# Sparse attention's logits with keys made once per head: hi and lo parts stacked on the partitions

## The chip, the cores and the metric

The kernel runs on one core of one Trainium2 chip. The metric is the device time of one execution in microseconds (us). TensorE multiplies matrices, VectorE and ScalarE work on its results in PSUM and on tiles in SBUF, GpSimd (POOL) on tiles in SBUF, and SyncE (SP) issues the DMAs. Each engine works through its own list of instructions in order; semaphores tie the lists together.

## The reference, cut to what matters

One layer of an encoder: 2048 tokens, width 1024, float32. A projection feeds three mixers (a sparse attention, a gated linear attention, a window attention); their outputs go through an output projection, and a gated feed-forward layer follows. The change is in the sparse attention. It picks 256 keys for each query by an index score, and attends to these in a latent space of 128:

```python
c_kv = rms_norm(c_kv, kv_norm)                                  # 2048 x 128
q_lat = einsum('bshd,rhd->bshr', q, w_uk) * HEAD_DIM ** -0.5    # 4 heads, 64 -> 128
score = einsum('bqhs,bqh->bqs', relu(einsum('bqhd,bsd->bqhs', qi, k_idx)), wi)
_, sel = top_k(where(admissible, score, -inf), 256)             # blocks of 128 queries
logits = einsum('bqhr,bqkr->bhqk', q_lat, c_kv[sel]) + bias     # bias by distance, 4 heads
p = softmax(where(valid, logits, -inf))
o = einsum('bshr,rhd->bshd', einsum('bhqk,bqkr->bqhr', p, c_kv[sel]), w_uv)
```

A logit is thus q . (w_uk^T c): the query can be taken to the latents (q w_uk^T), or the latents to keys of 64 numbers per head (c w_uk).

## The kernel before, in words

Products that need nearly full precision are made of packed parts: a number x becomes hi (rounded to the packed type) and lo = x - hi, and a product is hi.hi + lo.hi + hi.lo, three matmuls into one PSUM tile. Plain float32 operands take two passes of TensorE and stream their columns at half the rate.

The tokens go in four groups of 512. `dense()` is one thread of work: `pass1` for each group (projections of the sparse attention's inputs), `pass2` for each group (the two other mixers), then the feed-forward layer for groups 0 and 1, one group at a time (PSUM tiles `mf`). `dsa()` is the other thread: for each of 16 blocks of 128 queries `select` finds the 256th largest score by bisection (VectorE and ScalarE in turns), and `attend` attends. `merge` interleaves both threads in program order by the costs that they yield: the one that lags by its share of its total is taken next. `dsa`'s total is `SPEED` times a sum over the blocks of the larger of `select_cost` and `attend_cost`. The framework then orders each engine's list by its own estimate, near program order. When both threads are done, the feed-forward layer runs for groups 2 and 3 together, seven half products in place of eight (PSUM tiles `pf`).

In `attend` of block qb the keys are 0 to (qb+1)*128. The query's part `qa` is loaded from DRAM (L1238), taken to the latents by four products of plain type (L1242), and split to `lh` and `ll`. Per head the keys go in strips of at most 512 columns; the last strip is 256 wide and takes the bias `near`, which POOL adds to the mask (L1257) from the resident table `near_s`; beyond 128 keys the bias is one number per head, which cancels. A strip is three products (L1264 to L1266) and one instruction on VectorE that adds the mask and takes the least (L1268). ScalarE takes the exponential (L1272), TensorE turns it (L1281), and sums with the values `cv` (L1291).

`cTh` and `cTl` hold the latents' hi and lo parts, 128 partitions x 2048 each, made in `pass1` (L803, L804). `pers` holds what lives through the sparse attention, `gl` what ends with `pass2`, and `f1` opens its pools when `pass2` has ended. Weights are split once into hi and lo (L114, L117), stored, and loaded again by later groups (`load_halves`, L129 and L142), through five or six tiles `w`.

Of the kernel before, what the change touches and what calls it, by code (L numbers as in the profile page):

```python
# [19 lines left out]
P = 128  # L20
# [16 lines left out]
C_ID, C_GLA, C_BIT, C_POW, C_SWA, C_CAUS, C_REV, NC_ = 0, 128, 256, 288, 320, 576, 832, 960  # L37
# [47 lines left out]
def hybrid_encoder_kernel(ctx, tc, xT, w_in, w_out, w_g, w_u, w_d, vec, wuk, wuv, wg2,  # L85
# [10 lines left out]
    qaD = [dram.tile([2, P, G], F32, name=f"qaD{g}") for g in range(NG)]  # L96
# [4 lines left out]
    bD = dram.tile([8, NREL], F32, name="bD")  # L101

# [80 lines left out]
    def ffn(groups, pools, ps_f, ps_n, n_raw, n_w, n_act, n_lead, before, prepare=iter(())):  # L183
# [306 lines left out]
        def gate_up(f):  # L490
# [5 lines left out]
            for i, hs in enumerate(halves):  # L496
# [86 lines left out]
    with ExitStack() as mx:  # L583
# [48 lines left out]
        cs = pers.tile([P, C_SWA], F32, name="cs")  # L632
        ident = cs[:, C_ID:C_ID + P]
        wuk_s = pers.tile([P, 4, P], F32, name="wuk_s")
        wuv_s = pers.tile([P, 256], F32, name="wuv_s")
        bits = pers.tile([P, 32], I32, name="bits")

        def constants():
            nc.sync.dma_start(out=cs, in_=cst[:, 0:C_SWA])
# [6 lines left out]
        cTh = pers.tile([P, S], F32R, name="cTh")  # L646
        cTl = pers.tile([P, S], F32R, name="cTl")
# [4 lines left out]
        nsink = gl.tile([P, 4], F32, name="nsink")  # L652
        bias_s = gl.tile([P, 4, 256], F32, name="bias_s")
        near_s = pers.tile([P, 4, 256], F32, name="near_s")

        def bias_tables():
# [17 lines left out]
            for h in range(0, 8, 2):  # L674
# [8 lines left out]
                if h < 4:  # L683
                    A.copy(near_s[:, h:h + 2, :], pt.rearrange("p (h k) -> p h k", h=2))
# [81 lines left out]
        def pass1(g):  # L766
# [22 lines left out]
            for j in range(2):  # L789
# [5 lines left out]
                if j == 0:  # L795
# [28 lines left out]
                nc.sync.dma_start(out=qaD[g][j], in_=t)  # L824
# [94 lines left out]
        def gla_mix(g, j, bx):  # L919

            qe, ke, kd, vt, dec = (bx[n] for n in ("qe", "ke", "kd", "vt", "dec"))
            for t2 in range(2):
                pa = ps_mm()
                for u in range(2):
# [6 lines left out]
                                in1=cs[:, C_GLA:C_GLA + P].unsqueeze(1).to_broadcast([P, 4, P]),  # L931
# [174 lines left out]
        def select(qb, res):  # L1106
# [38 lines left out]
            def col(nm, dt=F32, n=1):  # L1145
                return sp.tile([P, n], dt, tag=nm, name=nm)
# [37 lines left out]
            e0, st, ps2, up = col("e0"), col("st", F32, 32), col("ps2", F32, 32), col("up")  # L1184
# [48 lines left out]

        def attend(qb, res):
# [3 lines left out]
            nc.sync.dma_start(out=qa[:, 0:256].rearrange("p (j t) -> p j t", j=2),  # L1238
                              in_=qaD[g].rearrange("j p t -> p j t")[:, :, q0:q0 + P])
# [15 lines left out]
            def logits(hd):  # L1255
                near = sp.tile([P, 256], F32, tag="near", bufs=N_NEAR, name="near")
                Q.tensor_add(near[:, 0:nw], x[:, far:nk], near_s[:, hd, 256 - nw:256])  # L1257
                lg = lgs[hd] = big()

                least = sp.tile([P, 8], F32, tag="least", name="least")  # L1260
# [222 lines left out]
```

## Time and profile before

| | |
|---|---|
| median of 3 runs | 2905.21 us (2900.52 to 2906.05) |
| the profiled execution's own time | 2909.43 us |
| its span | 2907.7 us |
| TensorE busy, share of the span | 2716.1 us, 93% |
| VectorE, ScalarE, POOL busy | 61%, 43%, 28% |
| mean granted clock of TensorE | 0.969 |
| moved by DMA | 471.08 MB, mean 162 GB/s |

A row of the timeline has the start, the time that the instruction took, the engine, the line, the operation, the tiles out<-in, rows*columns of the array that it uses, the shape of the moving operand, and its count; behind it, in brackets, the engine's idle time before it and what ended that. Matmuls overlap, so the time between two starts is what one costs. PE is TensorE, PEld its weight loads.

### The profile page before, as it was taken

To read this page: it belongs to the slowest core of one execution; us is meant where nothing else is said; L and a number is where in the kernel's file an instruction comes from. 1 tells how busy PE (TensorE), PEld (TensorE's weight loads), DVE (VectorE), ACT (ScalarE), POOL (GpSimd) and SP (SyncE) were. 2 spreads that over 40 slices of the span, in tenths; PEclk is the share of its full clock that TensorE was granted. 3 is DMA by queue.
4 is the path that set the end of the run, shared out by engine and by line. 5 is a ranking of instruction groups with operands and counts; after the bars stand their busy time and mean duration, and the time that the engine had idled before them with its cause. 6 is when DMAs were issued, how large, how long until landed. Compare 5 with 4: busy or idle time off the path is not lost. (4 is left out here: it accounts for less than half of the span.)

```text
span 2907.7 us, 37058 instructions
## 1 busy us (share of the span) xinstructions
PE 2716.1 (93%) x13136; PEld 2132.4 (73%) x13136; DVE 1782.3 (61%) x3662; ACT 1245.6 (43%) x2168; POOL 819.6 (28%) x666
## 2 busy tenths in 40 slices
PE   7888999999999989998988998999998999999998
PEld 5666767676776767776766786878776888888886
DVE  3787787787776767466367464464446544444445
ACT  4555664556555645454354442342433211112113
POOL 3113421010100354544442300000123443445440
PEclk8999999999999999999999999999999999999999
DMA  7655544243332666666657443444573443334432
GB/s 250 195 179 191 183 131 146 93 144 111 104 122 92 228 205 216 241 204 224 218 202 260 157 164 126 153 138 145 182 258 116 142 138 117 110 127 131 136 102 102
DMA packets 191114, 471.08 MB, mean 162 GB/s; under 512 B 19945, under 2 KB 51601, under 8 KB 190929
## 3 DMA queue, kind: packets, MB, share of 16 engines
q1 hardware_dynamic: 190928, 468.71, 48.8%
q8 instruction: 104, 1.70, 0.2%
q14 instruction: 82, 0.66, 0.1%
HBM read 341.61 MB, written 127.02 MB: 161 GB/s over the span
## 5 line engine op out<-in xcount | busy, mean ns | idle before, releaser
L117 POOL TENSOR_TENSOR w<-raw,w 128x512 fp32r<-128x512 f32 x272 | 367.2, 1361 | 596.7 <-ACT w L114 562.9
L1169 ACT ACTIVATE jd<-x,c 128x384 bf16<-128x384 f32 (+13 forms) x224 | 292.9, 1307 | 301.0 <-DVE c L1196 238.7
L201 PE MATMUL mf<-al,w 128*128 128x512 f32 x832 | 330.2, 398 | 9.6 <-DVE al L259 5.0
L199 PE MATMUL mf<-ah,w 128*128 128x512 f32 x832 | 332.7, 400 | 6.4 <-ACT ah L278 2.6
L1171 DVE TENSOR_SCALAR_CACHE_REDUCE jd<-x,c 128x384 bf16<-128x384 f32 (+13 forms) x224 | 331.0, 1477 | 6.9 <-DVE c L1180 0.5
L200 PE MATMUL mf<-ah,w 128*128 128x512 f32 x832 | 328.7, 396 | 0.0
L114 ACT CAST w<-raw 128x512 fp32r<-128x512 f32 x272 | 165.2, 617 | 364.3 <-PE pf L527 190.8
L370 PE MATMUL pf<-al,w 128*128 128x512 f32 x616 | 242.6, 394 | 6.6 <-POOL al L293 3.5
L368 PE MATMUL pf<-ah,w 128*128 128x512 f32 x616 | 242.3, 393 | 5.7 <-ACT ah L292 5.7
L740 PE MATMUL mm<-hh,w 128*128 128x512 f32 x576 | 241.7, 420 | 4.3 <-issue 2.0
L369 PE MATMUL pf<-ah,w 128*128 128x512 f32 x616 | 241.7, 393 | 0.0
L741 PE MATMUL mm<-hh,w 128*128 128x512 f32 x576 | 232.8, 404 | 0.0
L742 PE MATMUL mm<-hl,w 128*128 128x512 f32 x576 | 231.4, 402 | 0.0
L201 PEld LDWEIGHTS mf<-al,w 128*128 128x128 f32 x832 | 159.2, 191 | 47.0 <-DVE al L259 5.5
L199 PEld LDWEIGHTS mf<-ah,w 128*128 128x128 f32 x832 | 159.7, 192 | 40.4 <-issue 4.9
L528 DVE TENSOR_TENSOR x<-x,pf 128x512 f32<-128x512 f32 (+1 forms) x184 | 121.5, 664 | 106.9 <-PE pf L527 106.0
L200 PEld LDWEIGHTS mf<-ah,w 128*128 128x128 f32 x832 | 159.5, 192 | 32.1
L525 PE MATMUL mf<-fh,w 128*128 128x512 f32 x352 | 143.5, 408 | 17.7 <-ACT fh L114 6.9
L117 POOL TENSOR_TENSOR fl<-u,fh 128x512 fp32r<-128x512 f32 x44 | 58.1, 1320 | 321.1 <-ACT fh L114 321.1
L370 PEld LDWEIGHTS pf<-al,w 128*128 128x128 f32 x616 | 117.1, 190 | 34.2 <-POOL al L293 5.3
L526 PE MATMUL mf<-fh,w 128*128 128x512 f32 x352 | 140.7, 400 | 1.4 <-POOL w L117 1.4
L525 PE MATMUL pf<-fh,w 128*128 128x512 f32 (+1 forms) x368 | 141.1, 384 | 0.0
(299 smaller groups left out, 5914.0 us busy)
## 6 DMA issues: line engine op xcount, KB each, us to landing
w<-w SPq DMA_DIRECT2D x622, 512.0 KB, 3.5
raw<-in_w_g_dram SPq DMA_DIRECT2D x88, 256.0 KB, 3.6
raw<-in_w_u_dram SPq DMA_DIRECT2D x88, 256.0 KB, 3.4
xk<-in_xT_dram SPq DMA_DIRECT2D x64, 256.0 KB, 3.1
raw<-in_w_in_dram SPq DMA_DIRECT2D x44, 256.0 KB, 3.7
raw<-in_w_d_dram SPq DMA_DIRECT2D x44, 256.0 KB, 3.7
m<-mixT SPq DMA_DIRECT2D x32, 256.0 KB, 3.2
x<-in_xT_dram SPq DMA_DIRECT2D x32, 256.0 KB, 5.3
```

Source lines behind the costliest of these rows:

```text
L117: Q.tensor_sub(lo, src, hi.bitcast(F32))
L199: T.matmul(ps, a, act[k][0], start=(first and k == ks[0]), stop=False)
L200: T.matmul(ps, b, act[k][0], start=False, stop=False)
L201: T.matmul(ps, a, act[k][1], start=False, stop=(last and k == ks[-1]))
L368: T.matmul(ps, x, b[0], start=first, stop=False)
L369: T.matmul(ps, y, b[0], start=False, stop=False)
L370: T.matmul(ps, x, b[1], start=False, stop=last)
L525: T.matmul(ps, hi[:, os_], ah[:, hs], start=(j == 0), stop=False)
L740: T.matmul(ps, a, hh, start=(k == 0), stop=False)
L741: T.matmul(ps, b, hh, start=False, stop=False)
L1169: A.activation(jd, xs, AF.Sign, scale=-1.0, bias=c[:, 0:1], accum_out=cnt)
L1171: V.tensor_scalar(out=jd, in0=xs, scalar1=c[:, 0:1], scalar2=0.0, op0=ALU.is_ge, op1=ALU.add, accum_out=cnt)
```

## The change

The keys are made once: in `pass1`, per group, two products of plain type take the normed latents `cn` to keys of two heads each (64 partitions a head). The hi part of a head's keys goes to 64 partitions and the lo part to the other 64 of the same tile, `kt`, 1536 columns a head; the last group's go through DRAM (`k3D`) to `kt3`, which is loaded once the pools of `pass2` are closed. The query stands twice on the partitions. A strip is then two products: `lh` (the query's hi part on all 128 partitions) with the stacked keys, which gives hi.hi and hi.lo in one, and `ll` with the 64 partitions of hi alone. The products of L1242 go. The table of the near bias goes to DRAM, and each head of each block loads its piece. Beside that, tiles: the constants are laid out anew, `wuk_s`, `wuv_s` and the causal mask move to `gl`, the gate's product reuses its tile `s`, the stored sums of weights take tiles of the common tag `w`, three small tiles of `select` have one buffer. The costs that `attend` yields are smaller. Block 12 and later ones wait in the program until `kt3` is there, and the feed-forward thread until all blocks have attended.

```diff
@@ bias_tables
-                    A.copy(near_s[:, h:h + 2, :], pt.rearrange("p (h k) -> p h k", h=2))
+                    nr = gen_tile("nr")
+                    A.copy(nr, pt)
+                    nc.sync.dma_start(out=nearD[h // 2], in_=nr)
@@ pass1
-                    A.copy(cTh[:, g0:g0 + G], cn)
-                    V.tensor_sub(cTl[:, g0:g0 + G], cn, cTh[:, g0:g0 + G].bitcast(F32))
                 yield 5.2 - PART
                 ps = yield from proj(CH_QA + j, h)
                 if j == 0:
+                    for j2 in range(2):
+                        pk = ps_tr()
+                        T.matmul(pk, wuk_s[:, j2 * P:(j2 + 1) * P], cn, start=True, stop=True)
+                        for u in range(2):
+                            hd = 2 * j2 + u
+                            k_ = kt[:, hd, g0:g0 + G] if g < NG - 1 else gen_tile("k3").bitcast(F32R)
+                            rh, rl = (slice(i * 64, i * 64 + 64) for i in (u, 1 - u))
+                            A.copy(k_[rh], pk[rh])
+                            V.tensor_sub(k_[rl], pk[rh], k_[rh].bitcast(F32))
+                            if g == NG - 1:
+                                nc.sync.dma_start(out=k3D[hd], in_=k_.bitcast(F32))
@@ summed_halves, gate_up
-                w = pool.tile([P, 1024], F32R, tag="ws", bufs=1, name="ws")
+                w = pool.tile([P, 1024], F32R, tag="w", bufs=N_W, name="ws")
...
-                u = ft.tile([P, 512], F32, tag="u", bufs=2, name="u")
-                V.scalar_tensor_tensor(out=u, in0=s, scalar=0.5, in1=pu, op0=ALU.mult, op1=ALU.mult)
-                split(u, ah[:, hs], al[:, hs])
+                V.scalar_tensor_tensor(out=s, in0=s, scalar=0.5, in1=pu, op0=ALU.mult, op1=ALU.mult)
+                split(s, ah[:, hs], al[:, hs])
@@ attend
-            pq = ps_sc()
-            for hd in range(4):
-                T.matmul(pq[:, hd * P:(hd + 1) * P], wuk_s[:, hd, :], qa[:, (hd // 2) * P:(hd // 2 + 1) * P],
-                         start=True, stop=True)
+            nc.sync.dma_start(out=qa4[0:64], in_=qsrc)
+            nc.sync.dma_start(out=qa4[64:128], in_=qsrc)
...
-            A.activation(lh, pq, AF.Copy, scale=0.125)
-            V.scalar_tensor_tensor(out=ll, in0=pq, scalar=0.125, in1=lh.bitcast(F32), op0=ALU.mult, op1=ALU.subtract)
+            A.activation(lh, qa, AF.Copy, scale=0.125)
+            for u in range(2):
+                r = slice(u * 64, u * 64 + 64)
+                V.scalar_tensor_tensor(out=ll4[r, u::2], in0=qa4[r, u::2], scalar=0.125,
+                                       in1=lh4[r, u::2].bitcast(F32), op0=ALU.mult, op1=ALU.subtract)
+            while nk > N_KT and not kt3:
+                yield None
...
-                Q.tensor_add(near[:, 0:nw], x[:, far:nk], near_s[:, hd, 256 - nw:256])
+                nc.sync.dma_start(out=near[:, 0:nw],
+                                  in_=nearD[hd // 2][:, (hd % 2) * 256 + 256 - nw:(hd % 2 + 1) * 256])
+                Q.tensor_add(near[:, 0:nw], near[:, 0:nw], x[:, far:nk])
...
-                    T.matmul(ps[:, 0:w], lh[:, qs], cTh[:, k0:k0 + w], start=True, stop=False)
-                    T.matmul(ps[:, 0:w], ll[:, qs], cTh[:, k0:k0 + w], start=False, stop=False)
-                    T.matmul(ps[:, 0:w], lh[:, qs], cTl[:, k0:k0 + w], start=False, stop=True)
+                    for c0, k_ in keys(hd, k0, w):
+                        c1 = c0 + k_.shape[1]
+                        T.matmul(ps[:, c0:c1], lh[:, qs], k_, start=True, stop=False)
+                        T.matmul(ps[:, c0:c1], ll[hi, qs], k_[hi], start=False, stop=True)
...
-                    yield 0.9 * w / 512.0
+                    yield 0.6 * w / 512.0
...
-            return (qb + 1) * (0.9 + 1.0) + 1.5
+            return (qb + 1) * (0.6 + 1.0) + 0.6
@@ dense
+                k3p = f1.enter_context(tc.tile_pool(name="f1k", bufs=1))
+                kt3.append(k3p.tile([P, 4, G], F32R, name="kt3"))
+                nc.sync.dma_start(out=kt3[0].bitcast(F32), in_=k3D.rearrange("h p t -> p h t"))
...
                 yield from end
+                while len(attended) < NB:
+                    yield None
```

`keys(hd, k0, w)` returns the pieces of a strip: the columns of `kt` before 1536, and those of `kt3` behind.

On TensorE, in the second single feed-forward group, the start of block 14 stands so before the change (`mf` are dense products, `sc` the sparse attention's):

```order
L1242 MATMUL sc<-qa,wuk_s 128x128 x4
L199 MATMUL mf<-ah,w 128x512
L200 MATMUL mf<-ah,w 128x512
L201 MATMUL mf<-al,w 128x512
L199 MATMUL mf<-ah,w 128x512
L1264 MATMUL sc<-cTh,lh 128x512
L200 MATMUL mf<-ah,w 128x512
L201 MATMUL mf<-al,w 128x512
L1265 MATMUL sc<-cTh,ll 128x512
L1266 MATMUL sc<-cTl,lh 128x512
```

Now the strips of the last block, in the same stage (L201 to L203 are the dense products' lines now):

```order
L203 MATMUL mf<-al,w 128x512
L1298 MATMUL sc<-kt,lh 128x512
L1299 MATMUL sc<-kt,ll 128x512
L1298 MATMUL sc<-kt,lh 128x512
L1299 MATMUL sc<-kt,ll 128x512
L201 MATMUL mf<-ah,w 128x512
L202 MATMUL mf<-ah,w 128x512
L1298 MATMUL sc<-kt,lh 128x512
L1299 MATMUL sc<-kt,ll 128x512
L203 MATMUL mf<-al,w 128x512
```

A strip is a pair now, L1298 of 128 rows and L1299 of 64, mostly with dense products ahead and behind.

At the end of that stage TensorE's list before has the last block's turns and sums right ahead of the next stage's first product (`pf`):

```order
L1281 MATMUL tr<-cs,big 128x128 x4
L1310 MATMUL tr<-cs,dena 4x128
L1291 MATMUL o<-pT,cv 64x128
L1316 MATMUL tr<-dT,cs 64x128
L1291 MATMUL o<-pT,cv 64x128 x7
L1316 MATMUL tr<-dT,cs 64x128 x3
L199 MATMUL pf<-ah,w 128x512
```

and now the stage's own last products (L526 to L528) and a norm:

```order
L526 MATMUL mf<-fh,w 128x512
L527 MATMUL mf<-fh,w 128x512
L528 MATMUL mf<-fl,w 128x512
L236 MATMUL tr<-rs,ones 128x512
L201 MATMUL pf<-ah,w 128x512
```

The last block's sums stand some 120 rows earlier, among dense products.

On SP, at the load of block 12's index query (`qf`), the list before is:

```order
L142 DMA w_10086<-w 128x1024
L132 DMA raw<-in_w_u_dram 128x512
L1122 DMA qf<-qiD_69 64x4x128
L1123 DMA qf<-qiD_69 64x4x128
L142 DMA w_10093<-w 128x1024
```

and now:

```order
L134 DMA raw<-in_w_u_dram 128x512
L1286 DMA near<-nearD_80 128x256
L1138 DMA qf<-qiD_69 64x4x128
L144 DMA w_9876<-w 128x1024
```

A load of the near bias stands among the loads (`raw`) and stores (L144) of weights.

## Rows read from the trace of the kernel before

**Rows 1.** The page's first part: engines' busy us, share of the span, instructions

```profile
PE 2716.1 (93%) x13136; PEld 2132.4 (73%) x13136; DVE 1782.3 (61%) x3662; ACT 1245.6 (43%) x2168; POOL 819.6 (28%) x666
```

**Rows 2.** Busy time by stretch: PE, PEld, DVE, ACT, POOL; granted clock, DMA share, GB/s

```profile
0.00:250.00 250.00, 212.00 (x916) 156.33 (x917) 158.83 (x427) 132.96 (x280) 57.02 (x60) 0.92 0.65 206
250.00:1000.00 750.00, 706.05 (x3768) 523.48 (x3768) 585.57 (x1528) 440.86 (x878) 134.05 (x129) 0.97 0.42 135
1000.00:1570.00 570.00, 520.14 (x2502) 413.91 (x2501) 348.53 (x646) 293.31 (x451) 252.21 (x196) 0.96 0.64 221
1570.00:2085.00 515.00, 487.75 (x2422) 392.43 (x2421) 276.51 (x490) 181.34 (x248) 63.32 (x54) 0.97 0.47 155
```

**Rows 3.** Waits of PE: who for whom, us in total, times, longest

```profile
PE tr L1281 <- ACT big L1272: 20.6, 10, 7.3
...
PE sc L1264 <- DVE least L1268: 14.6, 9, 3.0
```

**Rows 4.** Timeline of PE: strips of 512 and of 256 columns

```profile
2061.61 0.40 PE L1265 MATMUL sc<-cTh,ll 128*128 128x512 f32 x1
2061.84 0.39 PE L1266 MATMUL sc<-cTl,lh 128*128 128x512 f32 x1
...
2066.45 0.28 PE L1265 MATMUL sc<-cTh,ll 128*128 128x256 f32 x1
2066.57 0.28 PE L1266 MATMUL sc<-cTl,lh 128*128 128x256 f32 x1
```

**Rows 5.** Line L1264, one product per strip: ns min/median/max, starts, shapes

```profile
L1264 PE MATMUL sc<-cTh,lh x192: 222/384/1169, 65.9 to 2095.4; 128*128 128x256 f32 x88, 128*128 128x512 f32 x72, 128*128 128x384 f32 x24, 128*128 128x128 f32 x8
```

**Rows 6.** Timeline of PE: one block's query taken to the latents

```profile
2051.94 1.05 PE L1242 MATMUL sc<-qa,wuk_s 128*128 128x128 f32 x8
2052.75 0.48 PE L199 MATMUL mf<-ah,w 128*128 128x512 f32 x1
```

**Rows 7.** Timeline of PE: a product of plain type, 512 columns, two passes

```profile
1601.09 1.10 PE L234 MATMUL tr<-rs,ones 128*128 128x512 f32 x2 [3.19 <-DVE rs L228]
1602.02 0.31 PE L1281 MATMUL tr<-cs,big 128*128 128x128 f32 x1
```

**Rows 8.** Timeline of PE: a product of 64 rows between dense ones

```profile
567.03 0.40 PE L742 MATMUL mm<-hl,w 128*128 128x512 f32 x1
567.36 0.70 PE L1026 MATMUL sc<-kct,qc 64*128 64x256 f32 x2
567.98 0.50 PE L740 MATMUL mm<-hh,w 128*128 128x512 f32 x1
568.32 0.39 PE L741 MATMUL mm<-hh,w 128*128 128x512 f32 x1
```

**Rows 9.** Timeline of PE: four passes of plain type, 128 rows, 256 columns

```profile
957.02 1.03 PE L926 MATMUL mm<-qe,ke 128*128 128x256 f32 x4
957.88 0.38 PE L1281 MATMUL tr<-cs,big 128*128 128x128 f32 x2
```

**Rows 10.** DMA issues: count, size of each, median us to landing

```profile
qa<-qaD SPq DMA_DIRECT2D x16, 128.0 KB, 3.4
```

**Rows 11.** Line L1257, the near bias: its instructions, and who waited for it

```profile
L1257 POOL TENSOR_TENSOR near<-mk,near_s x64: 427/678/1127, 69.9 to 2069.3; 128x256 f32<-128x256 bf16 x60, 128x128 f32<-128x128 bf16 x4
...
  DVE big L1268: 0.7, 2
```

**Rows 12.** Line L804: ns min/median/max, starts

```profile
L804 DVE TENSOR_TENSOR cTl<-cn,cTh x4: 681/693/857, 39.2 to 224.9; 128x512 fp32r<-128x512 f32 x4
```

**Rows 13.** Timeline of PE: the end of the second single feed-forward group

```profile
2087.65 0.39 PE L527 MATMUL mf<-fl,w 128*128 128x512 f32 x1
...
2098.82 1.13 PE L1281 MATMUL tr<-cs,big 128*128 128x128 f32 x8 [1.90 <-ACT big L1272]
...
2111.38 0.47 PE L199 MATMUL pf<-ah,w 128*128 128x512 f32 x1 [1.03 <-POOL al L259]
```

**Rows 14.** Timeline of SP: the next stage's first weights

```profile
2090.56 1.75 SPq L129 DMA_DIRECT2D w<-w  x4
```

More of the change, by code (lines that the diff above doesn't have):

```diff
@@ L35 @@
 V_MIX, V_FFN, V_FIN, V_KVN, V_BG, V_GN, V_SINK, NV = 0, 8, 16, 24, 25, 27, 31, 35
-C_ID, C_GLA, C_BIT, C_POW, C_SWA, C_CAUS, C_REV, NC_ = 0, 128, 256, 288, 320, 576, 832, 960
+C_ID, C_BIT, C_POW, C_GLA, C_SWA, C_CAUS, C_REV, NC_ = 0, 128, 160, 192, 320, 576, 832, 960
 CH_QA, CH_QI, CH_C, CH_M = 0, 2, 4, 5
@@ L95, in hybrid_encoder_kernel @@
     mixT = [dram.tile([KC, P, G], F32, name=f"mixT{g}") for g in range(NG)]
-    qaD = [dram.tile([2, P, G], F32, name=f"qaD{g}") for g in range(NG)]
+    qaD = [dram.tile([4, 64, G], F32, name=f"qaD{g}") for g in range(NG)]
     qiD = [dram.tile([4, 64, G], F32, name=f"qiD{g}") for g in range(NG)]
@@ L101, in hybrid_encoder_kernel @@
     bD = dram.tile([8, NREL], F32, name="bD")
+    nearD = [dram.tile([P, 512], F32, name=f"nearD{j}") for j in range(2)]
+    k3D = dram.tile([4, P, G], F32, name="k3D")
     const = ctx.enter_context(tc.tile_pool(name="const", bufs=1))
@@ L630, in big @@
             return bigp.tile([P, S], F32, tag="big", name="big")
-        cs = pers.tile([P, C_SWA], F32, name="cs")
+        cs = pers.tile([P, C_SWA - P], F32, name="cs")
         ident = cs[:, C_ID:C_ID + P]
-        wuk_s = pers.tile([P, 4, P], F32, name="wuk_s")
-        wuv_s = pers.tile([P, 256], F32, name="wuv_s")
+        wuk_s = gl.tile([P, 256], F32, name="wuk_s")
+        wuv_s = gl.tile([P, 256], F32, name="wuv_s")
         bits = pers.tile([P, 32], I32, name="bits")
         def constants():
-            nc.sync.dma_start(out=cs, in_=cst[:, 0:C_SWA])
+            nc.sync.dma_start(out=cs, in_=cst[:, 0:C_SWA - P])
+            nc.sync.dma_start(out=causal, in_=cst[:, C_GLA:C_GLA + P])
             nc.sync.dma_start(out=wuv_s, in_=wuv)
@@ L645, in hybrid_encoder_kernel @@
         cv = pers.tile([P, NB, 256], F32, name="cv")
-        cTh = pers.tile([P, S], F32R, name="cTh")
-        cTl = pers.tile([P, S], F32R, name="cTl")
+        N_KT = (NG - 1) * G
+        kt = pers.tile([P, 4, N_KT], F32R, name="kt")
+        kt3 = []
         ks = pers.tile([P, S], F32R, name="ks")
@@ L652, in hybrid_encoder_kernel @@
         nsink = gl.tile([P, 4], F32, name="nsink")
+        causal = gl.tile([P, P], F32, name="causal")
         bias_s = gl.tile([P, 4, 256], F32, name="bias_s")
-        near_s = pers.tile([P, 4, 256], F32, name="near_s")
         def bias_tables():
@@ L823, in pass1 @@
                 V.tensor_mul(t, ps, rs)
-                nc.sync.dma_start(out=qaD[g][j], in_=t)
+                nc.sync.dma_start(out=qaD[g][2 * j:2 * j + 2].rearrange("u d t -> (u d) t"), in_=t)
                 yield 5.2 - PART
@@ L930, in gla_mix @@
                                 in0=pa.rearrange("p (b i) -> p b i", i=P),
-                                in1=cs[:, C_GLA:C_GLA + P].unsqueeze(1).to_broadcast([P, 4, P]),
+                                in1=causal.unsqueeze(1).to_broadcast([P, 4, P]),
                                 op=ALU.mult)
@@ L1143, in select, with col @@
             Q.memset(x[0:64, nk - 64:nk], LOW)
-            def col(nm, dt=F32, n=1):
-                return sp.tile([P, n], dt, tag=nm, name=nm)
+            def col(nm, dt=F32, n=1, bufs=2):
+                return sp.tile([P, n], dt, tag=nm, bufs=bufs, name=nm)
             xs = x[:, 0:nk]
@@ L1232, in select_cost, with keys @@
             return 4 * nk / 512.0 + 4.0 * nk / 960.0 + 9 * (nk / 960.0 + 0.4) + 23 * (nk / 1000.0 + 0.6)
+        def keys(hd, k0, w):
+            k1, r = k0 + w, []
+            if k0 < N_KT:
+                r.append((0, kt[:, hd, k0:min(k1, N_KT)]))
+            if k1 > N_KT:
+                a = max(k0, N_KT)
+                r.append((a - k0, kt3[0][:, hd, a - N_KT:k1 - N_KT]))
+            return r
         def attend(qb, res):
@@ L1237, in attend @@
             qa = att_tile("qa")
-            nc.sync.dma_start(out=qa[:, 0:256].rearrange("p (j t) -> p j t", j=2),
-                              in_=qaD[g].rearrange("j p t -> p j t")[:, :, q0:q0 + P])
-            pq = ps_sc()
-            for hd in range(4):
-                T.matmul(pq[:, hd * P:(hd + 1) * P], wuk_s[:, hd, :], qa[:, (hd // 2) * P:(hd // 2 + 1) * P],
-                         start=True, stop=True)
+            qa4, qsrc = qa.rearrange("p (h t) -> p h t", h=4), qaD[g].rearrange("h d t -> d h t")[:, :, q0:q0 + P]
+            nc.sync.dma_start(out=qa4[0:64], in_=qsrc)
+            nc.sync.dma_start(out=qa4[64:128], in_=qsrc)
             lh = sp.tile([P, 512], F32R, tag="lh", bufs=1, name="lh")
             ll = sp.tile([P, 512], F32R, tag="ll", bufs=1, name="ll")
-            A.activation(lh, pq, AF.Copy, scale=0.125)
-            V.scalar_tensor_tensor(out=ll, in0=pq, scalar=0.125, in1=lh.bitcast(F32), op0=ALU.mult, op1=ALU.subtract)
+            A.activation(lh, qa, AF.Copy, scale=0.125)
+            lh4, ll4 = (t.rearrange("p (h t) -> p h t", h=4) for t in (lh, ll))
+            for u in range(2):
[4 more added lines that the diff above has]
+                yield None
             x = res[0]
@@ L1452, in _layout @@
     vec[:, V_SINK:V_SINK + 4] = f["sinks"][0][None, :]
-    wuk = np.zeros((P, 4, P), np.float32)
-    for h in range(4):
-        wuk[(h % 2) * 64:(h % 2) * 64 + 64, h, :] = f["w_uk"][0][:, h, :].T
     cst, oh = _constants()
```

5 lines of the change are left out of this document (3 added, 2 removed).

## The prediction

> **What bounds the kernel now.** I read the page's first part first: TensorE is busy for 93% of the span, no other engine for more than 61% [rows 1]. Then busy time by stretch, over the four stages in which the sparse attention runs beside dense work (first projections, second projections, two single feed-forward groups): 85, 94, 91 and 95% [rows 2]. The waits of TensorE come third: the longest entry is 20.6 us in ten pieces [rows 3]. So up to 2085 us the end is set by how long TensorE's own list takes; a saving on another engine is worth nothing there, and a microsecond on TensorE about 0.93 us, the mean share of these stages (1926 of 2085 us). The last 820 us (the double feed-forward group) hold no edited instruction.
>
> I read TensorE's cost from start to start in the timeline, since the durations shown there overlap: 512 columns of the packed type take 0.23 us, 256 take 0.12 [rows 4].
>
> **The change part by part.**
>
> *The third logits product goes.* It stands once per strip, 192 times: 72 of 512 columns, 24 of 384, 88 of 256, 8 of 128 [rows 5], together 69,632 columns, or 136 times 512. 136 x 0.23 = 31.3 us of TensorE less. The second product now contracts 64 rows instead of 128. I give that no gain: its 512 columns still have to stream.
>
> *The query's way to the latents goes.* Four products per block showed as eight passes, from 2051.94 us to the next dense product at 2052.75: 0.81 us [rows 6]. 16 x 0.81 = 13.0 us less.
>
> *The keys per head are made.* Two products of plain type and 512 columns per group, eight in all. One such took 0.93 us (1601.09 to 1602.02) [rows 7]: 7.4 us more. So far TensorE has 36.9 us less to do.
>
> *The shape of the array alternates.* This is the term that decides. The first product of a strip has 128 rows, the second 64, and the next instruction has 128 again. The kernel before has a product of 64 rows in its window attention, L1026, amid dense ones, and [rows 8] prices the way there and back: L742 starts at 567.03, L1026 at 567.36, which is 0.33 instead of 0.23. Its two passes of 256 columns of plain type then last until 567.98, 0.62 us; two such passes of 128 rows cost 0.43 (four from 957.02 to 957.88) [rows 9], so 0.19 more for two, 0.10 for one. The product after next starts 0.34 after its forerunner, again 0.11 too late. So a strip that has dense work behind it pays 0.10 + 0.10 + 0.11 = 0.31 us, one followed at once by the next strip or by short passes about 0.20. Bounds: 0.20 for all, and 0.40 (all of the 1.29 us from 567.03 to 568.32, less 0.89 for the same work without it). In the new instruction order there are 200 pairs (eight of the 192 strips are cut in two where the keys change tile). About 110 have two dense products behind them, the others the next strip or short passes: 110 x 0.31 + 90 x 0.20 = 52 us; bounds 40 and 80. A strip of 512 columns saves 0.23 us and pays 0.20 to 0.31; one of 256 saves 0.12 and pays the same.
>
> The Trainium skill (TensorEngine Tiling (Array Packing), Key Properties) says that to change the tiling mode, as against the tile alone, drains TensorE. The trace agrees as far as the late starts of [rows 8] go. Read to the letter, each of 400 changes costs what a product is still busy beyond its start-to-start time, 0.39 - 0.23 = 0.16 us by [rows 4]: 64 us instead of 52, inside the bounds above.
>
> Net on TensorE: -36.9 + 52 = +15 us, with the bounds from +3 to +43; times 0.93 it is +14.
>
> *The bias near the diagonal comes from DRAM.* 64 loads of 128 KB, on SP's queue, among the weight loads. The nearest load, the query's, lands after 3.4 us [rows 10]. The add on POOL was waited for by 0.7 us in all before [rows 11], so it has room, and in the new order SP issues a load well ahead of its use. What SP now waits for is that VectorE has read the tile two heads back; behind it stand weight loads, whose five or six tiles hold more than 10 us of dense work each way (a tile feeds 12 products, 2.7 us). I count nothing for the 63 later loads. The first must wait until the table has gone to DRAM and back, two landings instead of none while VectorE waits: between 0 and 7 us, I take 2. The query's second copy (16 more loads of 128 KB) lies beside its first: 0. Should that cover go, each late load costs up to 3.4 us (see the rivals).
>
> *Copies in the first projections.* Per group, four casts on ScalarE and four subtractions on VectorE of 64x512 take the place of one each of 128x512. The removed subtraction took 0.69 us [rows 12]; with as long for each new one, it is 12 x 0.69 = 8 us on either engine. In the first stage these are busy 159 and 133 of 250 us, so I count 0; TensorE could wait for a PSUM tile, 1 us per group at most. For the last group the four results go through DRAM: their stores and one 1 MB load are far from use (the keys are read first in block 12, long after).
>
> *The edits of tiles* (one tile less after the gate product, the stored weight sums through the common weight tiles, single buffers for three small columns, the two waits in the program) have one answer: their readers are many microseconds away, and in the order the two waits never hold anything up, since block 12 comes well inside the first feed-forward group. 0, and 5 us either way at the start of the second feed-forward group, where the stored sums stand between the norms.
>
> *The end of the sparse attention.* Its steps are now counted as shorter, so it runs earlier against the dense work. Before, the last dense product of the stage starts at 2087.65 and the next at 2111.38 [rows 13], 23.7 us in which the last block stands alone, with one gap of 1.90 before its transposes; by what its passes take amid dense work I estimate a third of that stretch as lost, 8 us (bounds 1.9 and 23.7). In the new order the last block ends some 120 rows ahead of the next stage's first product, and that loss goes. But what is late next stands there too: the next stage's first weights wait on SP for the last square sum on VectorE, and were issued at 2090.56 [rows 14]; with a landing of 3.4 us or more, TensorE would stand from 2087.9 to about 2094.5 with only a norm product to do. 8 lost before, 7 after: -1 us.
>
> **Sum.** 14 + 2 - 1 = +15 us. I take off 4 us, for drains that fall where TensorE would wait for VectorE anyway (14.6 us of [rows 3] stand before a strip's first product). The profiled execution took 2909.4 us, so 2920; the median of the runs is 4.2 us below the profiled one: 2916 us.
>
> **The rivals.**
>
> *The switch is free for a single pass* (faster). L1026 is of a type with two passes and two loads of weights; if that, not its 64 rows, makes the late starts, the change keeps its 36.9 us: x 0.93 = 34, less 1 for the end, plus 2: 2905 - 33 = 2872. For it: no row here shows a packed product of 64 rows. Against it: the start of the dense product after L1026 is late as well, and that one is packed.
>
> *Drains hidden in waits* (no change). If TensorE's 159 us without work in these stages take up half the net, and the end keeps its whole 8 us, it is 7 + 2 - 8 = +1: 2906. For it: the attention's chain through VectorE and ScalarE paces the strips. Against it: a drain stands between dense products, where nothing waits.
>
> *The near loads stand in SP's way* (slower still). SP issues in order; a near load that waits for VectorE holds the weights behind it, and POOL's add, now waiting for a landing, holds POOL's other work, as the low halves of operands. It decides once the add comes later than the head's last strip, that is in short heads. With 1 us for each of the 24 heads of the first six blocks: +24, so 2940. Against it: the loads stand early in the order.
>
> **How the numbers follow.** Forecast (2908 to 2925) 0.43, of which 0.08 lies within 0.2% of the time before; hidden drains 0.20, of which 0.17 within 0.2%, 0.03 faster; free switch 0.17, all faster; SP's queue or the high bound of the switch 0.20, slower. Within 0.2% (6 us, about what a measurement of this kernel can tell) thus 0.25, faster 0.20, slower 0.55. The range leaves out most of the free switch and the worst of the queue: 2888 to 2940; the likeliest case alone has 2908 to 2925.
>
> **What would show it.** The timeline of a strip between dense products: the 64-row product starts about 0.32 us after the 128-row one, the dense product as long after that, and the second dense one 0.34 later. TensorE's busy time up to the last stage grows slightly although its products are fewer by 232 (192 + 64 gone, 8 + 16 new). The last block's strips lie among dense products, and TensorE stands 5 to 8 us before the last stage's first product. VectorE's wait for the near tile stays under 10 us in all. If the starts after a 64-row product are 0.23 apart, the forecast is wrong and the time is near 2872; if SP's waits before near loads reach tens of microseconds and TensorE waits for weights behind them, it is wrong the other way.

## The result, and the profile after

The changed kernel takes 2947.09 us (median of 4 runs, 2945.27 to 2953.34), the kernel before 2905.52 beside it, so the medians are 41.6 us apart. The ratio over all runs, which is used from here on, is 1.0154 (95% interval 1.0140 to 1.0168), or 45 us. The forecast was slower, 2916 us, within 2888 to 2940: the side was right, the size was not, and the time lies outside the range.

The page's first part of the changed kernel (busy us, share of the span, instructions), whose span is 2943.6 us:

```profile
PE 2754.4 (94%) x12848; PEld 2097.6 (71%) x12848; DVE 1812.7 (62%) x3690; ACT 1249.6 (42%) x2180; POOL 829.4 (28%) x666
```

Against [rows 1] TensorE has 288 passes fewer and is busy 38.3 us longer. Its time without work (span less busy) is 189 us, 192 before. The forecast's net on TensorE was +15.

To see where the time is lost, both executions are cut at the same dense products: the start of the one with 750 ahead of it (soon after the first projections), of the one with 2000 ahead (near the end of the second projections), and of the double feed-forward group's first one. Busy time by stretch (PE, PEld, DVE, ACT, POOL; granted clock, DMA share, GB/s), first the kernel before:

```profile
0.00:321.71 321.71, 271.81 (x1196) 201.00 (x1197) 217.33 (x566) 172.38 (x357) 84.74 (x80) 0.93 0.64 205
321.71:899.83 578.12, 550.04 (x2985) 409.22 (x2983) 450.82 (x1199) 335.36 (x675) 81.76 (x89) 0.98 0.39 124
899.83:2111.38 1211.55, 1126.89 (x5585) 892.48 (x5583) 719.13 (x1362) 557.81 (x848) 347.00 (x275) 0.96 0.55 187
```

and the changed kernel:

```profile
0.00:341.09 341.09, 284.77 (x1154) 197.61 (x1155) 236.06 (x588) 180.38 (x374) 86.85 (x81) 0.92 0.63 204
341.09:932.66 591.57, 561.97 (x2902) 402.71 (x2901) 459.76 (x1208) 335.69 (x673) 81.25 (x89) 0.97 0.41 128
932.66:2141.75 1209.09, 1136.34 (x5420) 864.03 (x5419) 718.91 (x1356) 554.80 (x846) 348.65 (x270) 0.97 0.57 191
```

The first stretch is 19 us longer, the second 13, the third 2 shorter. Nearly all of the loss is made beside the projections; the spans of these two executions differ by 36 us, and the last 5 come behind the third stretch.

The timeline of TensorE at two strips between dense products (start, us, as in the rows before):

```profile
2048.22 0.39 PE L201 MATMUL mf<-ah,w 128*128 128x512 f32 x1
2048.45 0.40 PE L1298 MATMUL sc<-kt,lh 128*128 128x512 f32 x1
2048.78 0.50 PE L1299 MATMUL sc<-kt,ll 64*128 64x512 f32 x1
2049.21 0.50 PE L202 MATMUL mf<-ah,w 128*128 128x512 f32 x1
2049.55 0.39 PE L1298 MATMUL sc<-kt,lh 128*128 128x512 f32 x1
```

From start to start: 0.23, 0.33, 0.43, 0.34, where 0.23 is the price without a change of shape [rows 4]. Entering the 64 rows costs 0.10, leaving them 0.20, the product after next 0.11. The forecast had the outer two right and took 0.10 for leaving. Two strips in a row pay the same for each pair:

```profile
2040.93 0.39 PE L1298 MATMUL sc<-kt,lh 128*128 128x512 f32 x1
2041.25 0.49 PE L1299 MATMUL sc<-kt,ll 64*128 64x512 f32 x1
2041.67 0.50 PE L1298 MATMUL sc<-kt,lh 128*128 128x512 f32 x1
2042.11 0.50 PE L1299 MATMUL sc<-kt,ll 64*128 64x512 f32 x1
2042.54 0.50 PE L201 MATMUL mf<-ah,w 128*128 128x512 f32 x1
```

The third step (0.44) is the product after next and an entry in one.

Waits of TensorE in the changed kernel (who for whom, us, times, longest), the entries that answer to [rows 3] and to the forecast's other steps:

```profile
PE sc L1298 <- DVE least L1301: 9.9, 5, 5.5
PE mf L526 <- DVE x L529: 9.4, 7, 2.6
PE pf L201 <- DMA w<-w: 6.0, 2, 4.2
...
PE tr L1314 <- ACT big L1305: 3.9, 5, 2.3
```

The attention's own waits have shrunk (20.6 to 3.9 before the transposes, 14.6 to 9.9 before a strip), and a wait of dense products has grown (3.1 before), for VectorE's sums in the feed-forward layer.

The near bias, from the instructions of L1288 and who waits for them, and from POOL's waits:

```profile
L1288 POOL TENSOR_TENSOR near<-near,mk x64: 423/673/1801, 78.1 to 2057.5; 128x256 f32<-128x256 f32 x60, 128x128 f32<-128x128 f32 x4
...
  DVE big L1301: 2.7, 4
```

```profile
POOL near L1288 <- DMA near<-nearD: 157.2, 26, 20.2
```

The same add in the kernel before:

```profile
POOL near L1257 <- DVE least L1268: 155.5, 22, 34.0
```

POOL stands 157 us for the loads, but it stood as long for VectorE before, so the wait has only changed its name. VectorE waits 2.7 us for POOL (0.7 before, [rows 11]).

The end of the second single feed-forward group (timeline of TensorE), against [rows 13]:

```profile
2133.34 0.40 PE L528 MATMUL mf<-fl,w 128*128 128x512 f32 x1
2137.96 2.07 PE L236 MATMUL tr<-rs,ones 128*128 128x512 f32 x2 [4.22 <-DVE rs L230]
2141.75 0.76 PE L201 MATMUL pf<-ah,w 128*128 128x512 f32 x1 [1.72 <-DMA w<-w]
```

The last dense product comes 45.7 us later than before, the next stage's first one only 30.4 later: this end is 15 us shorter, as the last block no longer stands in it, and it has the 8 us with a norm product alone that the forecast described. What the forecast did not describe is the clock behind it, in the changed kernel and in the kernel before:

```profile
2141.75:2147.00 5.25, 5.25 (x13) 4.14 (x14) 4.26 (x3) 0.94 (x2) 4.22 (x3) 0.54 0.59 229
```

```profile
2111.38:2117.00 5.62, 5.62 (x25) 4.66 (x26) 4.64 (x3) 2.13 (x4) 4.09 (x3) 1.00 0.96 296
```

After those 8 us the granted clock is 0.54 (1 is 2.4 GHz, 0.5 is 1.2), and TensorE does 13 products where it did 25. So some of the 15 us is given back behind this end, and the rest of the loss was made earlier.

### The profile page after: what moved, and what is told of

Read it like the earlier page. It is cut to its first block, busy times and chain, and to the rows that moved or that the text cites. A ratio compares the mean times of both kernels' runs of the same rounds, so it can differ in the third digit from the quotient of the medians.

```text
span 2943.6 us, 36729 instructions
## 1 busy us (share of the span) xinstructions
PE 2754.4 (94%) x12848; PEld 2097.6 (71%) x12848; DVE 1812.7 (62%) x3690; ACT 1249.6 (42%) x2180; POOL 829.4 (28%) x666
## 4 chain that ended last, share of the span: by engine, by line
PE 42%; DVE 9%; issue 5%; ACT 4%; POOL 2%; DMA 1%; SPq 0%; POOLq 0%; ACTq 0%; DVEq 0%
PE pf L372 5%; PE pf L371 5%; PE pf L370 5%; DVE jd L1187 4%; PE mf L201 3%; PE mf L203 3%; PE mf L202 3%; PE pf L528 3%; PE pf L527 3%; PE pf L526 3%; ACT jd L1185 2%; PE mf L526 1%; PE mf L527 1%; PE mf L528 1%; PE o L1324 1%
## 5 line engine op out<-in xcount | busy, mean ns | idle before, releaser
L201 PE MATMUL mf<-ah,w 128*128 128x512 f32 x832 | 338.2, 407 | 4.0 <-DVE ro L997 2.3
L203 PE MATMUL mf<-al,w 128*128 128x512 f32 x832 | 330.4, 399 | 9.0 <-POOL al L261 5.0
L203 PEld LDWEIGHTS mf<-al,w 128*128 128x128 f32 x832 | 158.9, 191 | 49.1 <-POOL al L261 6.3
L201 PEld LDWEIGHTS mf<-ah,w 128*128 128x128 f32 x832 | 159.5, 192 | 45.5 <-issue 7.3
L119 POOL TENSOR_TENSOR fl<-s,fh 128x512 fp32r<-128x512 f32 x44 | 61.8, 1404 | 393.9 <-ACT fh L116 393.7
L526 PE MATMUL mf<-fh,w 128*128 128x512 f32 x352 | 145.5, 414 | 21.0 <-DVE x L529 9.4
L747 PEld LDWEIGHTS mm<-hh,w 128*128 128x128 f32 x576 | 110.1, 191 | 44.7 <-issue 17.9
```

Of the source, the lines that this page charges most:

```text
L119: Q.tensor_sub(lo, src, hi.bitcast(F32))
L201: T.matmul(ps, a, act[k][0], start=(first and k == ks[0]), stop=False)
L203: T.matmul(ps, a, act[k][1], start=False, stop=(last and k == ks[-1]))
L526: T.matmul(ps, hi[:, os_], ah[:, hs], start=(j == 0), stop=False)
L747: T.matmul(ps, a, hh, start=(k == 0), stop=False)
```

## The experiments

Each ran beside the kernel before on the same chip; ratios are to it, and 0.0010 of it is 2.9 us. The first theory was S, the shape at 0.39 us a pair; its rival N, the near loads. When both left a loss unexplained, three took their place: M (the costs that order the attention), K (the making of the keys) and T (the edits of tiles).

**The array's shape.** The second product on all 128 rows: the query's lo part is made for both halves (one instruction in place of two) and meets hi and lo of the keys, which adds lo.lo.

```diff
-                V.scalar_tensor_tensor(out=ll4[r, u::2], in0=qa4[r, u::2], ...
+            V.scalar_tensor_tensor(out=ll, in0=qa, scalar=0.125, in1=lh.bitcast(F32), ...
...
-                        T.matmul(ps[:, c0:c1], ll[hi, qs], k_[hi], start=False, stop=True)
+                        T.matmul(ps[:, c0:c1], ll[:, qs], k_, start=False, stop=True)
```

Expected: 

> The changed kernel, with the second product of a strip on all 128 rows (the query's lo part stands on both halves, so it gives lo.hi and lo.lo): no instruction of 64 rows is left in the sparse attention's logits, the columns are the same. Theory S (the change of the array's shape costs 0.39 us a pair, 0.09 to enter, 0.19 to leave and 0.11 on the product after next, and not the 0.20 to 0.31 of the forecast): 200 x 0.39 = 78 us of TensorE go, times 0.93 = 72, so about 2875 us (2865 to 2885). Theory N (the shape costs the 52 us forecast, the rest of the loss comes from the near loads on SP's queue): 52 x 0.93 = 48 go, about 2899. Theory 0 (the shape costs nothing, keys and loads make the whole loss): 2940 or more.

Measured: 2913.57 us, 1.0047 (1.0033 to 1.0061). Against the change's 1.0154 that is 31 us for the shape, not 72; and with TensorE's list now 37 us shorter than before by the forecast's count, 14 us are still lost. No theory had this. Its timeline shows that the shape's price itself is gone:

```profile
2046.74 0.40 PE L528 MATMUL mf<-fl,w 128*128 128x512 f32 x1
2046.98 0.39 PE L1293 MATMUL sc<-kt,lh 128*128 128x512 f32 x1
2047.21 0.40 PE L1294 MATMUL sc<-kt,ll 128*128 128x512 f32 x1
2047.45 0.39 PE L1293 MATMUL sc<-kt,lh 128*128 128x512 f32 x1
```

The reverse: 64 rows put into the kernel before.

```diff
-                    T.matmul(ps[:, 0:w], ll[:, qs], cTh[:, k0:k0 + w], start=False, stop=False)
+                    T.matmul(ps[:, 0:w], ll[0:64, qs], cTh[0:64, k0:k0 + w], start=False, stop=False)
```

Expected: 

> The kernel before, with the second of the three products of a strip contracting 64 rows in place of 128 (it leaves out half of lo.hi); nothing else is touched, and the columns are the same. Theory S: 192 strips x 0.39 = 75 us more on TensorE, times 0.93 = +70, about 2975 us (2960 to 2985). The forecast's price (0.20 to 0.31): 192 x 0.26 = 50, times 0.93 = +46, about 2952. Theory 0: 2905.

Measured: 2934.21 us, 1.0120 (1.0103 to 1.0136), +35 us. A strip of it between dense products, and the page's first part:

```profile
1996.82 0.39 PE L201 MATMUL mf<-al,w 128*128 128x512 f32 x1
1997.05 0.40 PE L1264 MATMUL sc<-cTh,lh 128*128 128x512 f32 x1
1997.37 0.50 PE L1265 MATMUL sc<-cTh,ll 64*128 64x512 f32 x1
1997.80 0.50 PE L1266 MATMUL sc<-cTl,lh 128*128 128x512 f32 x1
1998.14 0.40 PE L199 MATMUL mf<-ah,w 128*128 128x512 f32 x1
```

```profile
PE 2773.5 (95%) x13136; PEld 2131.8 (73%) x13136; DVE 1784.9 (61%) x3662; ACT 1245.9 (42%) x2168; POOL 819.6 (28%) x666
```

Its steps are again 0.32, 0.43 and 0.34, 0.40 more than three plain ones: the price is that of the shape, in a kernel with nothing else of the change. But 57 us more of busy time made the span (2934.5) 27 us longer; the time without work fell from 192 to 161, so about half of the added work took the place of time without work. The mean granted clock of this execution is 0.973, that of the kernel before 0.969.

**The near bias and the keys, alone on the kernel before.** First the table to DRAM and its 64 loads, as in the change's diff.

Expected: 

> The kernel before, with the bias near the diagonal written to DRAM and loaded for each head of each block, as the change does it, and nothing else of the change. Theory S: the loads lie beside other work, 2905 us (within 6). Theory N (a near load that waits for VectorE holds the weights behind it, and the add on POOL waits for a landing): +20 us or more, 2925 and above.

Measured: 2904.20 us, 1.0019 (1.0010 to 1.0027): 3 to 8 us. Theory N falls. The counter-test, on the kernel with 128 rows:

```diff
-                nc.sync.dma_start(out=near[:, 0:nw], in_=nearD[hd // 2]...
-                Q.tensor_add(near[:, 0:nw], near[:, 0:nw], x[:, far:nk])
+                Q.tensor_add(near[:, 0:nw], x[:, far:nk], kt[:, hd, 0:nw].bitcast(F32))
```

Expected: 

> The first kernel of this set (second product on 128 rows), with the near bias taken from a resident tile of other contents (the first keys stand in for the bias table, so the bias itself is left out) and so without its 64 loads and without the store of the table. Theory S: as the first kernel, within 6 us. Theory N: 20 us or more below it.

Measured: 2919.55 us, 1.0063 (1.0050 to 1.0076), against 1.0047 with the loads. Without them nothing is gained; this kernel leaves the bias itself out.

The keys, made and not used:

```diff
+                    for j2 in range(2):
+                        T.matmul(pk, wuk_s[:, j2, :], cn, start=True, stop=True)
...
+                            A.copy(k_[rh], pk[rh])
+                            V.tensor_sub(k_[rl], pk[rh], k_[rh].bitcast(F32))
+                            if g == NG - 1:
+                                nc.sync.dma_start(out=k3D[hd], in_=k_.bitcast(F32))
```

Expected: 

> The kernel before with the keys of the change made beside its own work: per group two products of plain type, four casts on ScalarE, four subtractions on VectorE, and for the last group four stores to DRAM. Nothing reads them (the weights in these two products are one head's each, so their contents are not the change's), and the latents' own hi and lo parts stay. Theory K: 10 us slower or more, as VectorE gets 16 x 0.69 = 11 us of work and the last group's stores stand in SP's way. Theories M and T: TensorE's 7.4 us at a weight of a half, about +4, 2904.

Measured: 2910.91 us, 1.0028 (1.0018 to 1.0038): +8 us (5 to 11), more than TensorE's share, and less than theory K's 10 except at the interval's upper end.

**What a microsecond of TensorE is worth.** The kernel before without its third product (L1266):

Expected: 

> The kernel before without the third product of a strip (it leaves out hi.lo), and nothing else: 31.3 us of TensorE work less. If a microsecond of TensorE is worth 0.93 of one, as forecast: -29, about 2871. If it is worth what the 64 rows in the kernel before gave (35 for 75 us, 0.46): -14, about 2886.

Measured: 2889.58 us, 0.9957 (0.9944 to 0.9969): -13 us (9 to 16) for 31.3, or 0.42 (0.29 to 0.52). The forecast's 0.93 is wrong by a factor of two.

**The costs that order the attention.** What is left of the diff is the smaller costs. They put back, on the kernel with 128 rows:

```diff
-                    yield 0.6 * w / 512.0
+                    yield 0.9 * w / 512.0
...
-            return (qb + 1) * (0.6 + 1.0) + 0.6
+            return (qb + 1) * (0.9 + 1.0) + 1.5
```

Expected: 

> The changed kernel with the second product on 128 rows, as in the first set (2913.6 us beside 2899.6 for the kernel before), and with the costs that the attention yields put back to those of before (0.9 for a strip, 1.9 for a block of keys and 1.5); nothing else. It has 37 us less of TensorE work than the kernel before and is 14 us slower. Theory M (the smaller costs let the attention's blocks, with their work on VectorE, run earlier against the projections, in a stretch that VectorE bounds): most of that loss goes, 2890 to 2900. Theory K (the making of the keys and their stores cost it) or theory T (the edits of tiles and waits): no change, about 2913.

Measured: 2892.53 us, 0.9962 (0.9950 to 0.9975). 25 us come back, and this version is 10 us faster than the kernel before. The smaller costs alone, on the kernel before:

Expected: 

> The kernel before with the attention's smaller costs of the changed one (0.6 for a strip, 1.6 for a block of keys and 0.6), and nothing else: the same instructions in another order. Theory M: 10 to 20 us slower, 2910 to 2920. Theories K and T: 2900, within 6.

Measured: 2936.24 us, 1.0115 (1.0102 to 1.0128): 33 us lost with the same instructions in another order, more than theory M had. And the change whole, with the costs of before:

Expected: 

> The change whole (64-row products too), but with the costs that the attention yields left as before (0.9, 1.9, 1.5). Theory M (the smaller costs lose about 25 us by the order that they give; the products of 64 rows lose about 31): 2892 + 31 = about 2923 us, a ratio of 1.007 to the kernel before. If the two losses overlap, less: a ratio near 1.000 or, the other way, 1.012.

Measured: 2917.88 us, 1.0068 (1.0054 to 1.0083), as expected. So the two losses add up: 1.0068 - 0.9962 is 31 us for the shape, 1.0154 - 1.0068 is 25 us for the order, the same as with the other order and the other shape. Each of these differences is good to about 6 us. The first parts of this kernel's page and of the one with 128 rows and the same costs (spans 2927.9 and 2891.6):

```profile
PE 2760.6 (94%) x12848; PEld 2108.3 (72%) x12848; DVE 1793.8 (61%) x3690; ACT 1252.4 (43%) x2180; POOL 818.7 (28%) x666
```

```profile
PE 2685.0 (93%) x12848; PEld 2095.6 (72%) x12848; DVE 1790.3 (62%) x3674; ACT 1251.4 (43%) x2180; POOL 819.2 (28%) x666
```

200 pairs of 64 rows are 75.6 us of busy time here and 36 us of span. That is 0.38 for each, but the two executions differ in the mean granted clock, 0.964 and 0.969, and at a lower clock the same work is busy for longer. The other pair of executions, the changed kernel (busy 2754.4 us, clock 0.967) and the one with 128 rows (span 2917.9 us, clock 0.964), has the clocks the other way round:

```profile
PE 2702.5 (93%) x12848; PEld 2100.8 (72%) x12848; DVE 1802.8 (62%) x3674; ACT 1247.4 (43%) x2180; POOL 828.5 (28%) x666
```

Here the 200 pairs are 51.9 us. Busy time multiplied by the mean clock, an estimate of the work at 2.4 GHz, puts them at 59 and 58 us.

**How the order loses.** The position of a block is the number of dense products ahead of its end. With the costs of before block 12 ends behind about 4080, block 14 behind 5520; with the smaller ones behind about 3990 and 5350, so two to three per cent earlier. The waits of TensorE in the kernel before with the smaller costs, and the same entry in the kernel before:

```profile
PE mf L525 <- DVE x L528: 10.2, 7, 2.3
```

```profile
PE mf L525 <- DVE x L528: 3.1, 1, 3.1
```

Dense products wait 7 us more for VectorE; in the change the entry was 9.4. It does not explain the 33 us, since the attention's own two waits of [rows 3] shrink by 14 us in the same pair (20.6 to 11.9 and 14.6 to 9.2). The order was then varied: costs raised, costs halfway, and smaller costs in blocks 0 to 7 alone.

Expected: 

> The best kernel so far (second product on 128 rows, costs as before: 0.9962 of the kernel before), with the costs raised instead (1.2 for a strip, 2.2 for a block of keys, 2.4), so that the attention's blocks come later against the dense work. If earlier is worse throughout (more waits for VectorE the earlier the blocks come): faster again, a ratio of 0.990 to 0.995. If only the positions matter (the order before was a good one among many): slower, 1.000 or above.

Expected: 

> The same kernel with costs halfway between those of before and of the change (0.75, 1.75, 1.05). If the time goes steadily with how early the blocks come: halfway between 0.9962 and 1.0047, a ratio of about 1.000. If single positions decide: anything from 0.993 to 1.010.

Expected: 

> The kernel before with the smaller costs for blocks 0 to 7 alone (0.6, 1.6, 0.6), which run beside the projections; the later blocks, beside the feed-forward groups, keep the costs of before. With smaller costs in all blocks it was 1.0115 of the kernel before, and its trace lags the one of before by 15 us at the end of the projections and by 24 at the last stage. Theory M, losses where they stand in that trace: about 60% of it, a ratio of 1.007. If the loss comes from the blocks beside the feed-forward groups: 1.000 to 1.002.

Measured: raised 1.0046 (1.0031 to 1.0060), halfway 1.0047 (1.0031 to 1.0062), blocks 0 to 7 alone 1.0082 (1.0069 to 1.0096). Neither later nor halfway is in between: it is no steady slope. Smaller costs in blocks 0 to 7, which end beside the projections, make about 70% of the loss that they make in all blocks; the later blocks move a little with them (block 14 ends behind about 5490), so the share is not theirs alone. With raised costs the end shows why later is no better (timeline of TensorE, and the stretch between as busy time):

```profile
2051.79 0.39 PE L528 MATMUL mf<-fl,w 128*128 128x512 f32 x1
...
2116.09 0.47 PE L201 MATMUL pf<-ah,w 128*128 128x512 f32 x1 [1.02 <-POOL al L261]
```

```profile
2052.00:2116.00 64.00, 41.47 (x287) 27.90 (x285) 26.60 (x56) 26.93 (x41) 12.90 (x10) 0.81 0.26 93
```

64 us in which the last blocks stand alone, TensorE 41 of them busy at a clock of 0.81; with the costs of before the same stretch is 23.9 us (2072.40 to 2096.27 in its timeline), as in [rows 13]. Then costs raised for the first 12, 14 or 10 blocks (1.2, 2.2, 2.4) and lowered for the rest (0.6, 1.6, 0.6), the last kernel doing it on the one before:

```diff
-                    yield 0.9 * w / 512.0
+                    yield (1.2 if qb < 12 else 0.6) * w / 512.0
```

Expected: 

> The changed kernel with the second product on 128 rows; costs raised (1.2, 2.2, 2.4) for blocks 0 to 11 and those of the change (0.6, 1.6, 0.6) for the last four, so that these catch up before the dense work ends. With raised costs throughout, the trace was 14 us ahead of the one with the costs of before until the last block, and lost 37 us there, where that block stood alone. If the early blocks' later place is what gains: 0.9962 less 0.003 to 0.005, a ratio of 0.991 to 0.993, 2877 to 2882 us. If the gain was work put off and no more: 0.996 or above.

Expected: 

> The same with the raised costs for blocks 0 to 13 and the change's for the last two. Their catching up is later and steeper: if the place of the last blocks beside the end of the dense work decides, slower than the one before it, 0.993 to 1.000; if the early places alone decide, the same ratio as that one.

Expected: 

> The same with the raised costs for blocks 0 to 9 and the change's for the last six: blocks 12 to 15 then end as early as or earlier than with the costs of before. If early places in the feed-forward groups lose as they did with the smaller costs throughout: 0.995 to 1.000; if the blocks beside the projections alone decide: 0.991 to 0.993.

Expected: 

> The kernel before with the raised costs for blocks 0 to 11 and the smaller for the last four; nothing else. If the order gains by itself, whatever the products: as much as beside the second product on 128 rows, a ratio of 0.995 to 0.997. If the order of before was already the best for it: 1.000 or above.

Measured: 1.0004 (0.9993 to 1.0015), 1.0017 (1.0007 to 1.0026), 0.9981 (0.9969 to 0.9992), and 1.0073 (1.0056 to 1.0090) on the kernel before. None is below 0.9962. Of seven orders of the same work with 128 rows the ratios run from 0.9962 to 1.0047. The order of before has the lowest of them on both kernels, though with 128 rows the third (0.9981) cannot be told from it: their intervals overlap. The first two lose at the end again: between the starts of the 5500th and the 5750th dense product they fall 11 and 22 us behind the kernel with the costs of before, the third 1.

## Why the prediction was wrong

**The step that failed first is the last term**, "Its steps are now counted as shorter, so it runs earlier against the dense work", at -1 us. The end went as told (TensorE 8 us with a norm product alone), but the step priced the new order at its end only. The order changed for most of the 16 blocks over 2090 us, and that cost 25 us here and 33 on the kernel before. No rival had it: a changed weight in the interleaving was taken as free where no row showed a wait.

**The shape** was mis-sized in two ways that partly cancel. The reading of [rows 8] gave 0.19 us for the two passes of L1026 and was split as "0.10 for one"; it is the price of leaving the 64 rows, paid once for one pass as for two. A pair costs 0.38 to 0.40 from start to start, and 200 of them 76 to 80 us, not 52. It holds for pairs in a row as for those before dense work; the distinction of 110 and 90 fell. But TensorE's busy time as a whole grew by 58 or 59 us at the full clock, near the 52, and the kernel lost 31 us by it, less than the 44 that the forecast had (52 x 0.93, less 4). That the total came out near is luck; where the 20 us between the starts and the busy time stay is not shown. The Trainium skill (TensorEngine Tiling (Array Packing), Key Properties) says that a change of the tiling mode drains TensorE. The late starts of the pairs shown agree with it; the forecast's reading of it gave 64 us, where the starts give 76 to 80.

**The worth of a microsecond**, "about 0.93 us", is 0.42 for work taken away and 0.4 to 0.6 for work added in the logits. The busy share says how much of a stretch is covered, not that the rest stays as it is: when the pairs of 64 rows came in, TensorE's time without work shrank by 26 us (215 to 189, with the costs of the change) and by 39 (207 to 167, with those of before). The clock moved as well: the mean granted clock over the runs is 0.9737 with the 64 rows in the kernel before, where the kernel before beside it has 0.9714, and 0.9684 without the third product, against 0.9704. So the clock rose with the added work and fell with the removed work; as an estimate (the difference times the span) that took 6 to 7 us off the loss and off the gain. The rival of the hidden drains was thus half right on the shape, where the forecast gave it 4 us. With 0.4, the work removed (31.3 and 13.0) brings some 18 us, not 41.

**The keys** cost 8 us as forecast (7.4 on TensorE). At the worth of 0.42 only 3 of these are TensorE's; where the rest comes from was not traced. **The near loads** cost 3 to 8 us on the kernel before, where 2 were taken; that they stand in SP's way for 20 us and more is refuted, since their removal brought nothing and VectorE waited 2.7 us for POOL. **The free switch** is refuted by the starts. The edits of tiles were not tried by themselves.

**The sum as measured:** all of the change but shape and order is -11 us (0.9962), the shape +31, the order +25, together +45. The three are successive differences, so they must add up to the whole; what shows shape and order to be separate is that each is the same in the other pair of kernels. Of the -11, the parts measured or scaled come to -13 (third product), -5 (13.0 at 0.42, not run by itself), +8 (keys) and +5 (near loads), -5 in all; 6 us stay unassigned; what the edits of tiles do is in them. The near loads may be nearer to 0 in the changed kernel, where taking them out gained nothing.

**Left open:** by what the order loses. With 128 rows 17.5 of the 26 us between the two executions are longer busy time of the same instructions (2685.0 and 2702.5 us); multiplied by the mean granted clocks (0.969 and 0.964) both are 2602 to 2605 us, so there the busy time is longer by the lower clock. On the kernel before the loss is by half busy time (2716 to 2730), at the same mean clock of 0.969. With 64 rows it is time without work (167 us with the costs of before, 189 with the smaller ones), but the first of these executions is the slowest of its six, at a clock of 0.964. The mean clock over the runs falls with the smaller costs in all three pairs: 0.9683 to 0.9657 with 128 rows, 0.9704 to 0.9692 on the kernel before, and 0.9690 to 0.9658 with 64 rows. As an estimate (the change in 1 less the clock, times the span) that is 8, 5 and 10 us at most. Whether the waits pull the clock down or come with it, and which stall makes how much, is not settled.

## What to carry to other kernels

Price a change of the array's shape from start to start, and as one price for in and out (the same here for one pass and for two); where half of the rows would be free, fill them (here with lo.lo) rather than narrow the product. A busy share of 93% does not make a saved microsecond worth 0.93: time one removed product first. Never change an interleaving's weights together with the work they describe: run the new work in the old order first, since the order alone can cost more than the work saves.

## What the runs showed of the hardware that was not expected

A single product of 64 rows among those of 128 costs 0.10 us on entering, 0.20 on leaving and 0.11 on the product after next, with 512 columns or with 256 (then 0.31 from its start to the next one, where 0.12 is the plain price), of plain type [rows 8] or packed. POOL stood for 157 us before loads from DRAM while all others together waited 4 us for its adds; it had stood 156 us before the same adds without the loads. Behind 8 us in which TensorE had one product to do, its granted clock was 0.54 for 5 us, and 512 columns took 0.43 us from start to start (2142.74 to 2143.17 in its timeline) in place of 0.23. The granted clock went with the order of the same instructions, by 0.001 to 0.003 of its mean. The same instructions in other orders differ by up to 33 us of 2903.
